# Seven block products for eight in the second MLP product of a two-layer trunk (one core, fp32 by hi/lo pairs)

## The chip, the cores and the metric

The kernel runs on one core of one Trainium2 chip. The metric is the time of one execution on the device, in microseconds, median of several runs.

## The reference, cut to what matters

A decoder trunk of two layers over 1024 tokens of width 1024, in float32. Layer 0 has a mixer (a linear recurrence beside stick-breaking attention), layer 1 a causal convolution module. Each layer ends in the MLP that the change is about; `D_FF` is 4096:

```
def sq_relu_mlp(h, w1, w2):
    a = jax.nn.relu(h @ w1)
    return (a * a) @ w2
...
        h = rms_norm(x, mlp_norm_g[layer])
        x = x + sq_relu_mlp(h, mlp_w1[layer], mlp_w2[layer])
```

The attention masks its strictly causal triangle by adding -1e30 to the scores of the diagonal block before the sigmoids.

## The kernel before, in words

**Precision.** Every large product is computed from operands split into a high part (`fp32r`, written by ScalarE's copy, lines 104 and 125) and a low part (source minus high part, VectorE's subtraction, lines 105 and 126). One product is then three matmuls: low x high, high x low, high x high (`mm3`, lines 157 to 159).

**Tiling.** The tokens go in two chunks of 512. The first MLP product (`m1`) takes a block `f` of 128 of the 4096 hidden columns: weights of two blocks come in one transfer of 1 MB (`col_units`, line 114), 8 blocks of depth with three matmuls each (24 matmuls, all 128x512) fill one PSUM bank, ScalarE applies relu and square (lines 252, 254, 255) and VectorE makes the low part (line 256). The result has hidden columns on the partitions and 512 tokens along the row. The second product (`m2`) takes groups of `G` = 4 hidden blocks and one half `h` of the 1024 output columns: 1 MB of `mlp_w2` (line 139), split in two pieces of 128x1024, and for each of the 4 token tiles 4 x 3 matmuls into one bank, which VectorE adds to the residual `x` (line 240). One MLP of one chunk is 32 `m1` and 16 `m2`, that is 768 + 768 matmuls. There are four: `a0` and `b0` (layer 0, chunks 0 and 1), `a1` and `b1` (layer 1).

**Buffers.** Pool `hp` has 48 slots of 128x512 (2 KB per partition); the residuals take 16 and the normed input of one chunk (high and low) 16. Pool `wp` has 2 slots for raw weights (8 KB), 4 for high and 4 for low parts (4 KB each). Pool `lp` (8 slots, 2.1 KB) is open throughout, `p1` belongs to the mixer and is followed in the same space by `p2` (tags `b` and `c`), which the rest of the kernel uses. PSUM has 8 banks: 2 for transposes (`ps`), and 6 in `ps1` (mixer) or `ps2` (4 `mm`, 2 `m1`).

**Order.** The kernel is written with a tile framework: the instructions are listed in program order, a list scheduler with its own model of times puts them in order on each engine and assigns buffer slots, and every semaphore wait follows from that. VectorE's depthwise convolution (480 instructions, line 648) is issued in small portions behind other VectorE work (`paced`); it lies beside `b0`, the convolution module and `a1`. The main order (lines 731 to 764) is: `m1` of `a0` twice, norm of chunk 1, the rest of `a0`, `b0` with the start of the convolution module, the convolution module of both chunks, `a1`, the norm of chunk 1, `finish(0)` (final norm and output of chunk 0), `b1`, `finish(1)`. All loads are issued from the SP queue. GpSimd issues none.

**Lines that the change touches:** pools (46, 600 to 609), identity and mask (74 to 81), `mlp` (243), the mask matmul (501), `finish` (704), the main order (730 to 764).

Of the kernel before, what the change touches and what calls it, by code (L numbers as in the profile page):

```python
# [15 lines left out]
P = 128  # L16
# [15 lines left out]
def tile_hybrid_trunk(  # L32
# [13 lines left out]
    lp = ctx.enter_context(tc.tile_pool(name="lp", bufs=8))  # L46
# [8 lines left out]
    def hf(name):  # L55
        return ht(name, F32)
# [2 lines left out]
        return ht(name, dt)  # L59

    def lt(name):
        return lp.tile([P, HALO + C], F32, tag="l", name=name)

    def mm_ps(name):
        return mmp[0].tile([P, C], F32, tag="mm", bufs=mmp[1], name=name)
# [11 lines left out]
    make_identity(nc, ident_b)  # L77
    mask = cp.tile([P, P], BF16, name="mask")
    Q.memset(mask, 0.0)
    Q.affine_select(out=mask, in_=mask, pattern=[[-1, P]], compare_op=ALU.is_gt,  # L80
                    fill=-1e30, base=0, channel_multiplier=1)

    cp.tile([P, 16], F32, name="pad_cp")
    mhalf = cp.tile([P, 1], F32, name="mhalf")
# [155 lines left out]
            paced(V.tensor_tensor(xt[t][h], acc, xt[t][h], op=ALU.add), 1.5)  # L240


    def mlp(layer, hT, xt, name):
# [20 lines left out]
        order = [(m1, f) for f in range(G)]  # L264
        for g in range(NG):
# [6 lines left out]
    NG = FF // (G * P)  # L272


    w_in = ev_w_in[0]
    y = [[None] * KT for _ in range(NCH)]
    dp = ctx.enter_context(tc.tile_pool(name="dp", bufs=1, space=bass.MemoryType.DRAM))
    with tc.tile_pool(name="p1", bufs=1) as p1, tc.tile_pool(name="ps1", bufs=1, space=PSUM) as ps1:
        mmp = (ps1, 2)

        def qt(name):
            return p1.tile([P, C], F32R, tag="q", bufs=8, name=name)
# [197 lines left out]
        def attention(c, hp, q1, q2, ks):  # L480
            av = ps1.tile([P, C], F32, tag="av", bufs=1, name=f"av{hp}{c}")
            order = None
            for tt in range(TT):
                n = (c * TT + tt + 1) * P
                carry = [None, None]
                hi_s = n
                while hi_s > 0:
                    lo_s = (hi_s - 1) // C * C
                    w = hi_s - lo_s
                    nb = w // P  # L490
                    diag = hi_s == n
                    wts = []
                    for j in range(2):
                        nm = f"{c}{hp}{tt}{j}{lo_s}"
                        z = ps1.tile([P, C], F32, tag="z", bufs=3, name=f"z{nm}")
                        ts_, k_ = slice(tt * P, (tt + 1) * P), ks[lo_s // C][j]
                        with tc.high_priority(offset=1000):
                            T.matmul(z[:, :w], q1[j][:, ts_], k_[:, :w], start=True, stop=False)
                            T.matmul(z[:, :w], q2[j][:, ts_], k_[:, :w], start=False, stop=not diag)
                            if diag:  # L500
                                T.matmul(z[:, w - P:w], ident_b, mask, start=False, stop=True)

                        ke = at(f"ke{nm}")
                        with tc.high_priority(offset=1000):
                            A.activation(ke[:, :w], z[:, :w], AF.Sigmoid, scale=-0.125)
                            A.activation(z[:, :w], z[:, :w], AF.Sigmoid, scale=0.125)
                        ini = 1.0 if diag else carry[j]
                        if diag:
                            Q.memset(ke[:, w:w + 1], 1.0)
                        else:  # L510
                            Q.tensor_copy(ke[:, w:w + 1], ini)
                        V.tensor_tensor_scan(ke[:, :w][:, ::-1], ke[:, :w][:, ::-1], ke[:, :w][:, ::-1],
                                             ini, op0=ALU.mult, op1=ALU.bypass)
                        if lo_s > 0:
                            carry[j] = sp.tile([P, 1], F32, tag="carry", bufs=6, name=f"ca{nm}")
# [81 lines left out]
        for h in range(NH):  # L597
            out_proj((1,), 1, h)

    p2 = ctx.enter_context(tc.tile_pool(name="p2", bufs=1))  # L600
    p2.tile([P, 96], F32, tag="pad", bufs=1, name="pad_p2")
    ps2 = ctx.enter_context(tc.tile_pool(name="ps2", bufs=1, space=PSUM))
    mmp = (ps2, 4)

    def bt(name, dt=F32):
        return p2.tile([P, C], dt, tag="b", bufs=11, name=name)

    def ct(name):
        return p2.tile([P, C], F32, tag="c", bufs=9, name=name)


    halo = cp.tile([P, KT, HALO], F32, name="halo")
# [89 lines left out]
        rows_into_x(s[kg * 4:kg * 4 + 4], ws, h, x[c], f"q2{c}{kg}{h}")  # L702

    def finish(c):
        fg = [ct(f"fg{c}{h}") for h in range(NH)]
        for h in range(NH):
            nc.sync.dma_start(fg[h], final_g[h * C:(h + 1) * C].rearrange("(a d) -> a d", a=1).to_broadcast((P, C)))
        for t in range(TT):
            o = [ct(f"fo{c}{t}{h}") for h in range(NH)]
# [24 lines left out]
    steps(a0)  # L734
# [59 lines left out]
```

## Time and profile before

| | |
|---|---|
| Time, median of 3 runs | 2208.8 us (2208.58 to 2209.05) |
| Time of the profiled execution | 2208.25 us |
| Its span (first to last instruction) | 2206.5 us |
| TensorE matmul busy | 2158.0 us (98%), 10180 matmuls |
| TensorE weight load busy (beside the matmuls) | 1764.2 us (80%) |
| VectorE busy | 1412.0 us (64%) |
| ScalarE busy | 957.6 us (43%) |
| GpSimd busy | 104.2 us (5%) |
| DMA | 199.24 MB, mean 90 GB/s |
| Mean granted TensorE clock | 0.993 |

Busy shares are means over stages with different limits. Matmuls are pipelined, so the time that one takes from its engine is read from the distance between the starts of two, not from its duration.

### The profile page before, as it was taken

The numbers are of one execution on the slowest core, as the hardware profiler recorded it, in microseconds if no ns is written. First come the engines' busy times: TensorE is split into PE (matmuls) and PEld (weight loads), VectorE is DVE, ScalarE is ACT, GpSimd is POOL, SyncE is SP. The second block draws the span as 40 slices with busy tenths as digits, with TensorE's granted clock in tenths as the row PEclk, the third lists the DMA queues.
The fourth block names the chain that finished last, engine by engine and source line by source line (L and its number), as shares of the span: only waits on it lengthen the run. The fifth ranks groups of instructions, "written<-read, shape, count | busy, mean of one in ns | idle before, by whom it ended". The sixth has DMA issues, their size and how long they took to land.

```text
span 2206.5 us, 25861 instructions
## 1 busy us (share of the span) xinstructions
PE 2158.0 (98%) x10180; PEld 1764.2 (80%) x10180; DVE 1412.0 (64%) x1934; ACT 957.6 (43%) x1513; POOL 104.2 (5%) x296
## 2 busy tenths in 40 slices
PE   7999888999999999999999999999999999999998
PEld 5877666788888888888888888788888888888887
DVE  5386868975433435489899664999896555444344
ACT  4466766645333334333333463333333535333332
POOL 1000000000000002000000000300000001000000
PEclk9999989999999999999999999999999999999999
DMA  4110102212323322332232222223232234222232
GB/s 161 58 54 24 53 25 91 101 59 78 100 90 99 110 96 92 109 96 96 91 100 96 96 96 83 86 95 100 87 103 91 94 105 144 96 96 96 96 96 76
DMA packets 172009, 199.24 MB, mean 90 GB/s; under 512 B 5648, under 2 KB 120688, under 8 KB 171888
## 3 DMA queue, kind: packets, MB, share of 16 engines
q1 hardware_dynamic: 171872, 197.59, 27.6%
q8 instruction: 80, 1.31, 0.2%
q14 instruction: 41, 0.34, 0.1%
q10 hardware_dynamic: 16, 0.00, 0.0%
HBM read 190.23 MB, written 7.34 MB: 90 GB/s over the span
## 4 chain that ended last, share of the span: by engine, by line
PE 91%; DVE 4%; ACT 3%; issue 1%; DMA 0%; POOL 0%; DVEq 0%; SPq 0%; POOLq 0%; ACTq 0%
PE m_a L157 5%; PE m_a L159 5%; PE o_a L159 5%; PE m_b L159 5%; PE m_a L158 5%; PE m_b L157 5%; PE o_a L157 5%; PE o_a L158 5%; PE m_b L158 5%; PE o_b L159 5%; PE o_b L157 5%; PE o_b L158 5%; PE av L529 1%; PE o_q L157 1%; PE o_q L158 1%; PE o_q L159 1%
## 5 line engine op out<-in xcount | busy, mean ns | idle before, releaser
L648 DVE SCALAR_TENSOR_TENSOR cv<-u,dwT,cv 128x512 f32<-128x512 f32 x480 | 340.6, 756 | 0.2
L157 PE MATMUL o_a<-wh_w2a,al_a 128*128 128x512 f32 x512 | 199.6, 390 | 0.0
L158 PE MATMUL o_a<-wl_w2a,ah_a 128*128 128x512 f32 x512 | 199.5, 390 | 0.0
L157 PE MATMUL o_b<-wh_w2b,al_b 128*128 128x512 f32 x512 | 199.4, 390 | 0.0
L159 PE MATMUL o_b<-wh_w2b,ah_b 128*128 128x512 f32 x512 | 199.4, 389 | 0.0
L158 PE MATMUL o_b<-wl_w2b,ah_b 128*128 128x512 f32 x512 | 199.3, 389 | 0.0
L159 PE MATMUL o_a<-wh_w2a,ah_a 128*128 128x512 f32 x512 | 198.9, 389 | 0.0
L125 ACT CAST wh_w1b<-raw_w1b 128x1024 fp32r<-128x1024 f32 x64 | 67.3, 1052 | 211.9 <-PE o_b L159 168.6
L125 ACT CAST wh_w1a<-raw_w1a 128x1024 fp32r<-128x1024 f32 x64 | 67.3, 1053 | 206.2 <-PE o_a L159 162.8
L105 DVE TENSOR_TENSOR wl_w2a<-raw_w2a,wh_w2a 128x1024 fp32r<-128x1024 f32 x64 | 78.3, 1224 | 121.9 <-ACT wh_w2a L104 121.9
L105 DVE TENSOR_TENSOR wl_w2b<-raw_w2b,wh_w2b 128x1024 fp32r<-128x1024 f32 x64 | 80.9, 1264 | 115.9 <-ACT wh_w2b L104 115.8
L240 DVE TENSOR_TENSOR xr<-o_a,xr 128x512 f32<-128x512 f32 x128 | 87.8, 688 | 76.5 <-PE o_a L159 76.1
L240 DVE TENSOR_TENSOR xr<-o_b,xr 128x512 f32<-128x512 f32 x128 | 88.0, 688 | 71.3 <-PE o_b L159 70.9
L252 ACT ACTIVATE r_a<-m_a 128x512 f32<-128x512 f32 x64 | 38.4, 599 | 170.5 <-PE m_a L159 170.5
L159 PEld LDWEIGHTS o_b<-wh_w2b,ah_b 128*128 128x128 f32 x512 | 96.1, 188 | 19.9
L158 PEld LDWEIGHTS o_b<-wl_w2b,ah_b 128*128 128x128 f32 x512 | 96.1, 188 | 19.9
L159 PEld LDWEIGHTS o_a<-wh_w2a,ah_a 128*128 128x128 f32 x512 | 96.1, 188 | 19.9
L157 PEld LDWEIGHTS o_a<-wh_w2a,al_a 128*128 128x128 f32 x512 | 96.1, 188 | 19.8
L158 PEld LDWEIGHTS o_a<-wl_w2a,ah_a 128*128 128x128 f32 x512 | 96.1, 188 | 19.8
L157 PEld LDWEIGHTS o_b<-wh_w2b,al_b 128*128 128x128 f32 x512 | 96.1, 188 | 19.8
L252 ACT ACTIVATE r_b<-m_b 128x512 f32<-128x512 f32 x64 | 38.4, 600 | 168.9 <-PE m_b L159 168.9
L126 DVE TENSOR_TENSOR wl_w1b<-raw_w1b,wh_w1b 128x1024 fp32r<-128x1024 f32 x64 | 78.0, 1221 | 36.0 <-ACT wh_w1b L125 35.6
(538 smaller groups left out, 5319.5 us busy)
## 6 DMA issues: line engine op xcount, KB each, us to landing
raw_w1a<-in_mlp_w_dram SPq DMA_DIRECT2D x32, 1024.0 KB, 5.1
raw_w2a<-in_mlp_w_dram SPq DMA_DIRECT2D x32, 1024.0 KB, 5.0
raw_w1b<-in_mlp_w_dram SPq DMA_DIRECT2D x32, 1024.0 KB, 5.1
raw_w2b<-in_mlp_w_dram SPq DMA_DIRECT2D x32, 1024.0 KB, 4.9
raw_pw<-in_od_pw_w_dram SPq DMA_DIRECT2D x32, 512.0 KB, 4.5
raw_q<-in_od_pw_w_dram SPq DMA_DIRECT2D x8, 1024.0 KB, 5.1
raw_wo<-in_ev_w_out_dram SPq DMA_DIRECT2D x6, 768.0 KB, 5.1
xa<-in_x_dram SPq DMA_DIRECT2D x16, 256.0 KB, 5.2
```

What stands on the lines that cost most here:

```text
L105: paced(V.tensor_tensor(lo, raw, hi.bitcast(F32), op=ALU.subtract), 1)
L125: A.copy(hi, srcs[i])
L126: paced(V.tensor_tensor(lo, srcs[i], hi.bitcast(F32), op=ALU.subtract), 2)
L157: T.matmul(acc, ll, rh, start=(i == 0), stop=False)
L158: T.matmul(acc, lh, rl, start=False, stop=False)
L159: T.matmul(acc, lh, rh, start=False, stop=(i == n - 1))
L240: paced(V.tensor_tensor(xt[t][h], acc, xt[t][h], op=ALU.add), 1.5)
L252: A.activation(r, acc, AF.Relu)
L529: ins = T.matmul(av[j * 64:j * 64 + 64, tt * P:(tt + 1) * P], vt[lo_s // P + b][:, hc:hc + 64], wts[j][:, b * P:(b + 1) * P], start=(diag ...
L648: waiting.append(lambda k=k, m=m: V.scalar_tensor_tensor(cv[m], u[m][:, k:k + C], dwT[:, k * KT + m:k * KT + m + 1], cv[m], op0=ALU.mult, ...
```

## The change

1. `mlp7` computes the second product of the MLP over eight hidden blocks at a time as a 2 x 2 x 2 block product with seven products instead of eight (a Strassen-Winograd scheme). The rows are the first and second 256 tokens of the chunk, the depth is the even and the odd hidden blocks, the columns are the two halves of the output. Each of the seven products is 2 token tiles x 4 depth blocks x 3 matmuls. It runs for three groups of `a0` (hidden blocks 0 to 23; the last 8 stay as they were, by `mlp(..., g0=6)`) and for all four groups of `b1`.
2. Sums of activation blocks (`s1` to `s4`) are made by VectorE, each then split high/low into slots of two wide tiles, `sh` and `sl`. Three sums of weight blocks are needed: `w11+w12`, `w12+w22` and `w11+w12+w22` are made by DMAs issued from GpSimd that add to a loaded tile (`accum_op`), and `w21` is added to the last of them by VectorE. Each operand is split while the product before runs (`ws`, `nx`).
3. Products accumulate in PSUM across products; after each one VectorE adds its bank to, or subtracts it from, one block of `x`.
4. Pools: `pa`/`psa` (strassen) replace `lp` + `p1`/`p2` and the `ps1`/`ps2` banks while they are open, so there are three changes of pools in place of one. `finish` takes its tiles from `hp`.
5. The identity and the mask are `fp32r` tiles, made through a float32 tile and a VectorE copy; the mask matmul is fp32r in place of bf16.

```diff
-    ident = cp.tile([P, P], F32, name="ident")
-    make_identity(nc, ident)
-    ident_b = cp.tile([P, P], BF16, name="ident_b")
-    mask = cp.tile([P, P], BF16, name="mask")
...
+    ident_r = cp.tile([P, P], F32R, name="ident_r")
+    ident = ident_r.bitcast(F32)
+    mask = cp.tile([P, P], F32R, name="mask")
+    for t_, fill in ((ident_r, None), (mask, -1e30)):
+        raw_c = wp.tile([P, P], F32, tag="wl", bufs=4, name="raw_c")
...
+        V.tensor_copy(t_, raw_c)
...
+    def mlp7(layer, hT, xt, name, pa, psa, groups):
+        w1, w2 = mlp_w1[layer], mlp_w2[layer]
+        def pair(f, n):
+            un = col_units(w1, f * P, (f + 1) * P, f"w1{n}")
+            lo = pa.tile([P, 7 * B2], F32R, tag="sl", bufs=4, name=f"sl{n}")
+            hi = pa.tile([P, 7 * B2], F32R, tag="sh", bufs=4, name=f"sh{n}")
+            ev, od, sa, sb = [hf(f"r{i}_{n}") for i in range(4)]
+            (a21, a11), (a22, a12), (s1, s3), (s2, s4) = [(r[:, :B2], r[:, B2:]) for r in (ev, od, sa, sb)]
+            def parts(r, s0):
+                sl = slice(s0 * B2, s0 * B2 + r.shape[1])
+                A.copy(hi[:, sl], r)
+                V.tensor_tensor(lo[:, sl], r, hi[:, sl].bitcast(F32), op=ALU.subtract)
+            for i, r in enumerate((ev, od)):
+                acc = m1_ps(f"m1_{n}{i}")
+                colmm(acc, un(i), hT)
+                A.activation(r, acc, AF.Relu)
+                A.activation(r, r, AF.Square)
+                if i == 0:
+                    V.tensor_tensor(s3, a11, a21, op=ALU.subtract)
+                    parts(a11, 0)
+            V.tensor_tensor(s1, a21, a22, op=ALU.subtract)
+            V.tensor_tensor(s2, s1, a11, op=ALU.subtract)
+            V.tensor_tensor(s4, a12, s2, op=ALU.add)
+            for r, s0 in ((od, 1), (sa, 3), (sb, 5)):
+                parts(r, s0)
+            return hi, lo
+        def w_rows(g, odd, h, nm):
...
+                t_ = hf(f"{nm}{name}{g}{k}")
+                nc.sync.dma_start(t_, w2[f * P:(f + 1) * P, h * C:(h + 1) * C])
...
+        def w_add(ts, g, odd, h):
+            for k in range(4):
+                f = 8 * g + 2 * k + odd
+                Q.dma_start(ts[k], w2[f * P:(f + 1) * P, h * C:(h + 1) * C], accum_op=ALU.add)
+        def w_split(ts, nm):
...
+                for j in range(2):
+                    js = slice(j * C, (j + 1) * C)
+                    A.copy(hi[:, js], ts[2 * i + j])
+                    V.tensor_tensor(lo[:, js], ts[2 * i + j], hi[:, js].bitcast(F32), op=ALU.subtract)
...
+        def product(banks, acts, slot, ws, first, into):
+            for t in range(2):
...
+                    T.matmul(banks[t], lo[:, ts], rh, ...)
+                    T.matmul(banks[t], hi[:, ts], rl, ...)
+                    T.matmul(banks[t], hi[:, ts], rh, ...)
+                for row, h, op in into:
+                    x_ = xt[(2 if row == 1 else 0) + t][h]
+                    V.tensor_tensor(x_, x_, banks[t], op=op)
...
+        for g in groups:
+            acts = [pair(8 * g + 2 * p, f"{n}{p}") for p in range(3)]
+            t1 = w_rows(g, 0, 0, "w11")
+            ws = w_split(t1, f"w11{n}")
+            w_add(t1, g, 0, 1)
+            t2 = w_rows(g, 1, 1, "t2")
+            w_add(t2, g, 0, 0)
+            w_add(t2, g, 0, 1)
+            acts.append(pair(8 * g + 6, f"{n}3"))
+            ba, bb = bank(f"pa_{n}", "sa"), bank(f"pb_{n}", "sb")
+            nx = w_split(t1, f"t1{n}")
+            w22 = w_rows(g, 1, 1, "w22")
+            product(ba, acts, 0, ws, True, [(1, 0, ALU.add)])
+            ws, nx = nx, w_split(t2, f"t2{n}")
+            t3 = w_rows(g, 0, 1, "w12")
+            w_add(t3, g, 1, 1)
+            product(bb, acts, 3, ws, True, [(2, 1, ALU.add)])
+            ws, nx = nx, w_split(w22, f"w22{n}")
+            w21 = w_rows(g, 1, 0, "w21")
+            product(ba, acts, 5, ws, False, [(1, 1, ALU.subtract)])
+            ws, nx = nx, w_split(t3, f"t3{n}")
+            for k in range(4):
+                V.tensor_tensor(t2[k], t2[k], w21[k], op=ALU.add)
+            product(bb, acts, 6, ws, False, [(1, 1, ALU.add)])
+            ws, nx = nx, w_split(w21, f"w21{n}")
+            product(ba, acts, 4, ws, False, [(2, 1, ALU.subtract)])
+            ws, nx = nx, w_split(t2, f"t4{n}")
+            bc = bank(f"pc_{n}", "sb")
+            product(bc, acts, 2, ws, True, [(1, 0, ALU.add)])
+            product(ba, acts, 1, nx, False, [(2, 0, ALU.add)])
...
-                                T.matmul(z[:, w - P:w], ident_b, mask, start=False, stop=True)
+                                T.matmul(z[:, w - P:w], ident_r, mask, start=False, stop=True)
...
-    a0 = mlp(0, hm[0], x[0], "a0")
+    strassen(0, hm[0], x[0], "a0", range(3))
+    mid = ExitStack()
...
+    a0 = mlp(0, hm[0], x[0], "a0", 6)
     steps(a0, -1)
...
     finish(0)
-    b1 = mlp(1, h2b, x[1], "b1")
-    steps(b1)
+    mid.close()
+    strassen(1, h2b, x[1], "b1", range(4))
     finish(1)
```

## Rows read from the trace of the kernel before

**Rows 1.** The page: span, busy time and instructions of each engine.
```profile
span 2206.5 us, 25861 instructions
PE 2158.0 (98%) x10180; PEld 1764.2 (80%) x10180; DVE 1412.0 (64%) x1934; ACT 957.6 (43%) x1513; POOL 104.2 (5%) x296
```

**Rows 2.** Stretches: us, busy us and (instructions) per engine, clock, DMA share, GB/s.
```profile
100.00:500.00 400.00, 377.51 (x2169) 290.81 (x2168) 308.19 (x451) 256.52 (x498) 23.77 (x126) 0.97 0.18 60
506.00:855.00 349.00, 348.28 (x1553) 288.77 (x1554) 147.19 (x175) 132.84 (x193) 4.70 (x12) 1.00 0.30 97
1850.00:2180.00 330.00, 330.00 (x1457) 273.27 (x1456) 135.33 (x155) 120.94 (x162) 3.25 (x6) 1.00 0.30 99
```

**Rows 3.** Waits of TensorE, 506 to 2190 us: total us, times, longest.
```profile
PE nps_ma L214 <- DVE hl_ma L220: 2.9, 2, 2.7
PE m_a L157 <- ACT hh_m L219: 0.9, 1, 0.9
```

**Rows 4.** TensorE's timeline in `b1`: start, duration, the 25 starts of one `m2` half.
```profile
1964.92 0.39 PE L157 MATMUL o_b<-wh_w2b,al_b 128*128 128x512 f32 x1
...
1970.36 0.39 PE L157 MATMUL o_b<-wh_w2b,al_b 128*128 128x512 f32 x1
```

**Rows 5.** VectorE and ScalarE by line, 1850 to 2190 us: count, busy us, mean ns.
```profile
L240 DVE TENSOR_TENSOR xr<-o_b,xr 128x512 f32<-128x512 f32 x60 | 41.4, 690 | 58.2 <-PE o_b L159 58.0
L126 DVE TENSOR_TENSOR wl_w1b<-raw_w1b,wh_w1b 128x1024 fp32r<-128x1024 f32 x30 | 36.6, 1221 | 25.1 <-ACT wh_w1b L125 25.1
L256 DVE TENSOR_TENSOR al_b<-r_b,ah_b 128x512 fp32r<-128x512 f32 x32 | 22.1, 691 | 27.6 <-ACT r_b L255 27.6
L254 ACT ACTIVATE ah_b<-r_b 128x512 fp32r<-128x512 f32 x32 | 20.1, 630 | 0.2
```

**Rows 6.** VectorE by line, the whole span: a tensor_tensor of 256 columns.
```profile
L517 DVE TENSOR_TENSOR ke<-z,ke 128x256 f32<-128x256 f32 x16 | 6.6, 421 | 1.1
```

**Rows 7.** VectorE's timeline in `b1`, around the start at 1964.92 of an `m2`.
```profile
1950.96 1.23 DVE L105 TENSOR_TENSOR wl_w2b<-raw_w2b,wh_w2b 128x1024 fp32r<-128x1024 f32 x1 [4.92 <-ACT wh_w2b L104]
1955.81 1.23 DVE L105 TENSOR_TENSOR wl_w2b<-raw_w2b,wh_w2b 128x1024 fp32r<-128x1024 f32 x1 [2.96 <-ACT wh_w2b L104]
1967.84 0.69 DVE L240 TENSOR_TENSOR xr<-o_b,xr 128x512 f32<-128x512 f32 x1
1968.45 0.68 DVE L256 TENSOR_TENSOR al_b<-r_b,ah_b 128x512 fp32r<-128x512 f32 x1
```

**Rows 8.** The page: DMA issues, KB each, median us from issue to landing.
```profile
raw_w2b<-in_mlp_w_dram SPq DMA_DIRECT2D x32, 1024.0 KB, 4.9
xa<-in_x_dram SPq DMA_DIRECT2D x16, 256.0 KB, 5.2
out_dram<-fo SPq DMA_DIRECT2D x16, 256.0 KB, 2.0
```

**Rows 9.** TensorE's timeline in the mixer: the mask matmul, and eight fp32 transposes.
```profile
439.29 0.34 PE L499 MATMUL z<-ks,q 128*128 128x384 f32 x1
439.47 0.23 PE L501 MATMUL z<-mask,ident_b 128*128 128x128 bf16 x1
439.51 0.47 PE L498 MATMUL z<-ks,q 128*128 128x512 f32 x1
494.84 1.03 PE L214 MATMUL nps_m<-ident,xn_m 128*128 128x128 f32 x8
495.63 0.48 PE L157 MATMUL o_wo<-wh_wo,y13l 128*128 128x512 f32 x1
```

**Rows 10.** Weight loads in the mixer, by line: count, busy us, mean ns.
```profile
L498 PEld LDWEIGHTS z<-ks,q 128*128 128x128 f32 x96 | 18.8, 196 | 9.6 <-DVE ks L564 3.8 <-DVE ke L517 2.3 <-PE z L499 0.6
L501 PEld LDWEIGHTS <-ident_b 128*128 128x128 bf16 x64 | 6.3, 99 | 7.6 <-issue 6.8
```

**Rows 11.** The end of the chain of waits: start, us, engine, tile, line.
```profile
2190.61 0.24 PE o_b L159
2190.88 0.70 DVE xr L240
...
2199.07 0.67 DVE xr L240
2199.82 0.63 ACT fo L186
```

More of the change, by code (lines that the diff above doesn't have):

```diff
@@ L61, in lt @@
     def lt(name):
-        return lp.tile([P, HALO + C], F32, tag="l", name=name)
+        return lpp[0].tile([P, HALO + C], F32, tag="l", bufs=8, name=name)
     def mm_ps(name):
@@ L71, in tr_ps @@
         return ps.tile([P, C], F32, tag="tr", bufs=2, name=name)
-    ident = cp.tile([P, P], F32, name="ident")
-    make_identity(nc, ident)
-    ident_b = cp.tile([P, P], BF16, name="ident_b")
-    make_identity(nc, ident_b)
-    mask = cp.tile([P, P], BF16, name="mask")
-    Q.memset(mask, 0.0)
-    Q.affine_select(out=mask, in_=mask, pattern=[[-1, P]], compare_op=ALU.is_gt,
-                    fill=-1e30, base=0, channel_multiplier=1)
+    ident_r = cp.tile([P, P], F32R, name="ident_r")
[3 more added lines that the diff above has]
+        raw_c = wp.tile([P, P], F32, tag="wl", bufs=4, name="raw_c")
+        if fill is None:
+            make_identity(nc, raw_c)
+        else:
+            Q.memset(raw_c, 0.0)
+            Q.affine_select(out=raw_c, in_=raw_c, pattern=[[-1, P]], compare_op=ALU.is_gt,
+                            fill=fill, base=0, channel_multiplier=1)
+        V.tensor_copy(t_, raw_c)
     cp.tile([P, 16], F32, name="pad_cp")
@@ L240, in rows_into_x, with mlp @@
             paced(V.tensor_tensor(xt[t][h], acc, xt[t][h], op=ALU.add), 1.5)
-    def mlp(layer, hT, xt, name):
+    def mlp(layer, hT, xt, name, g0=0):
         acts, units = {}, {}
@@ L263, in mlp @@
         NF = FF // P
-        order = [(m1, f) for f in range(G)]
-        for g in range(NG):
+        order = [(m1, f) for f in range(g0 * G, (g0 + 1) * G)]
+        for g in range(g0, NG):
             n = (g + 1) * G
@@ L272, in tile_hybrid_trunk, with bank @@
     NG = FF // (G * P)
+    B2 = 2 * P
+    def mlp7(layer, hT, xt, name, pa, psa, groups):
[25 more added lines that the diff above has]
+        def w_rows(g, odd, h, nm):
+            ts = []
+            for k in range(4):
+                f = 8 * g + 2 * k + odd
+                t_ = hf(f"{nm}{name}{g}{k}")
+                nc.sync.dma_start(t_, w2[f * P:(f + 1) * P, h * C:(h + 1) * C])
+                ts.append(t_)
+            return ts
+        def w_add(ts, g, odd, h):
+            for k in range(4):
+                f = 8 * g + 2 * k + odd
+                Q.dma_start(ts[k], w2[f * P:(f + 1) * P, h * C:(h + 1) * C], accum_op=ALU.add)
+        def w_split(ts, nm):
+            res = []
+            for i in range(2):
+                hi = wp.tile([P, 1024], F32R, tag="wh", bufs=4, name=f"wh_{nm}{i}")
+                lo = wp.tile([P, 1024], F32R, tag="wl", bufs=4, name=f"wl_{nm}{i}")
+                for j in range(2):
+                    js = slice(j * C, (j + 1) * C)
+                    A.copy(hi[:, js], ts[2 * i + j])
+                    V.tensor_tensor(lo[:, js], ts[2 * i + j], hi[:, js].bitcast(F32), op=ALU.subtract)
+                    res.append((hi[:, js], lo[:, js]))
+            return res
+        def product(banks, acts, slot, ws, first, into):
+            for t in range(2):
+                ts = slice(slot * B2 + t * P, slot * B2 + (t + 1) * P)
+                for i, ((hi, lo), (rh, rl)) in enumerate(zip(acts, ws)):
+                    T.matmul(banks[t], lo[:, ts], rh, start=(first and i == 0), stop=False, skip_group_check=not first)
+                    T.matmul(banks[t], hi[:, ts], rl, start=False, stop=False, skip_group_check=not first)
+                    T.matmul(banks[t], hi[:, ts], rh, start=False, stop=(i == 3), skip_group_check=not first)
+                for row, h, op in into:
+                    x_ = xt[(2 if row == 1 else 0) + t][h]
+                    V.tensor_tensor(x_, x_, banks[t], op=op)
+        def bank(nm, tag):
+            return [psa.tile([P, C], F32, tag=tag, bufs=2, name=f"{nm}{t}") for t in range(2)]
+        for g in groups:
+            n = f"{name}{g}"
+            acts = [pair(8 * g + 2 * p, f"{n}{p}") for p in range(3)]
[18 more added lines that the diff above has]
+            ws, nx = nx, w_split(t3, f"t3{n}")
+            for k in range(4):
+                V.tensor_tensor(t2[k], t2[k], w21[k], op=ALU.add)
[6 more added lines that the diff above has]
+            product(ba, acts, 1, nx, False, [(2, 0, ALU.add)])
@@ L277, in tile_hybrid_trunk @@
     dp = ctx.enter_context(tc.tile_pool(name="dp", bufs=1, space=bass.MemoryType.DRAM))
-    with tc.tile_pool(name="p1", bufs=1) as p1, tc.tile_pool(name="ps1", bufs=1, space=PSUM) as ps1:
+    lpp = [None]
+    with tc.tile_pool(name="lp1", bufs=1) as lp1, tc.tile_pool(name="p1", bufs=1) as p1, \
+            tc.tile_pool(name="ps1", bufs=1, space=PSUM) as ps1:
         mmp = (ps1, 2)
+        lpp[0] = lp1
         def qt(name):
@@ L598, in tile_hybrid_trunk @@
             out_proj((1,), 1, h)
[L600 to L603, printed above, removed]
+    pp = [None]
     def bt(name, dt=F32):
-        return p2.tile([P, C], dt, tag="b", bufs=11, name=name)
+        return pp[0].tile([P, C], dt, tag="b", bufs=11, name=name)
     def ct(name):
-        return p2.tile([P, C], F32, tag="c", bufs=9, name=name)
+        return pp[0].tile([P, C], F32, tag="c", bufs=9, name=name)
     halo = cp.tile([P, KT, HALO], F32, name="halo")
@@ L704, in finish @@
     def finish(c):
-        fg = [ct(f"fg{c}{h}") for h in range(NH)]
+        fg = [hf(f"fg{c}{h}") for h in range(NH)]
         for h in range(NH):
@@ L708, in finish @@
         for t in range(TT):
-            o = [ct(f"fo{c}{t}{h}") for h in range(NH)]
+            o = [hf(f"fo{c}{t}{h}") for h in range(NH)]
             rs = rstd_of(x[c][t], o[0], f"f{c}{t}")
@@ L730, in tile_hybrid_trunk, with strassen @@
     hm.append(None)
-    a0 = mlp(0, hm[0], x[0], "a0")
+    def strassen(layer, hT, xt, name, groups):
+        nonlocal mmp
+        with tc.tile_pool(name=f"pa{name}", bufs=1) as pa, tc.tile_pool(name=f"psa{name}", bufs=1, space=PSUM) as psa:
+            mmp = (psa, 2)
+            pa.tile([P, 96], F32, tag="pad", bufs=1, name=f"pad_{name}")
+            mlp7(layer, hT, xt, name, pa, psa, groups)
+    strassen(0, hm[0], x[0], "a0", range(3))
+    mid = ExitStack()
+    lpp[0] = mid.enter_context(tc.tile_pool(name="lp2", bufs=1))
+    pp[0] = mid.enter_context(tc.tile_pool(name="p2", bufs=1))
+    pp[0].tile([P, 96], F32, tag="pad", bufs=1, name="pad_p2")
+    mmp = (mid.enter_context(tc.tile_pool(name="ps2", bufs=1, space=PSUM)), 4)
+    a0 = mlp(0, hm[0], x[0], "a0", 6)
     steps(a0, -1)
```

1 line of the change is left out of this document (removed).

## The prediction

> **What bounds the kernel now.** I read the page's first lines, then the stretches, then TensorE's waits, then single rows for the prices. TensorE is busy for 98% of the span [rows 1], but a busy matmul engine can hide pauses, so the stretches decide: the two stages that the change rewrites, `a0` (506 to 855 us) and `b1` (1850 to 2180 us), have TensorE busy for 348.28 of 349.00 and 330.00 of 330.00 us, at a granted clock of 1.00 [rows 2], which is the 2.4 GHz level. The reader should see beside it that VectorE is busy for 147 and 135 us there, ScalarE for 133 and 121, GpSimd for 5 and 3: 40% at most. The waits agree: from 506 to 2190 us TensorE waits twice, 3.8 us in all [rows 3]. So in both stages the time is the count of matmuls times their distance. That distance is (1970.36 - 1964.92) / 24 = 0.2267 us [rows 4]; the duration of 0.39 us in the same rows is not it. What the change takes from TensorE there it takes from the end, as long as the other engines and the transfers keep up.
>
> **The change part by part.** *Matmuls.* Eight hidden blocks cost 2 x 2 x 4 x 4 x 3 = 192 matmuls in `m2`; seven products cost 7 x 2 x 4 x 3 = 168. They have the same shape and operands of the same type, so I price them the same. Seven groups save 7 x 24 = 168 matmuls, 168 x 0.2267 = **-38.1 us**. All of it lies on the path. The count should read 10180 - 168 = 10012.
>
> *VectorE and ScalarE in a group.* TensorE needs (192 + 168) x 0.2267 = 81.6 us for a group, 43.5 for the first products and 38.1 for the seven products, 5.44 for each. VectorE has per group 8 low parts of `w1` (1.22 us each), 28 of 128x512 for weights and 12 for activations (0.69), 4 of 256 columns, 16 sums of 256 columns (0.42), 14 adds into `x` (0.69) and 4 for the last weight sum (0.69) [rows 5, 6]: 9.8 + 27.6 + 1.7 + 6.7 + 9.7 + 2.8 = 58.3 us of 81.6. The share rises from 41% to 71%, still hidden on average. Inside the seven products it is tighter: 28 + 14 + 4 operations of 0.69 are 31.7 us, the sums and low parts of the last pair 3 x 0.42 + 3 x 0.69 = 3.3, the first two `w1` units of the next group 2.4: 37.5 of 38.1 us. Durations overlap a little (one starts 0.61 us after the start of another that lasts 0.69 [rows 7]); at 0.63 instead of 0.69 it is 34.6, 91%. ScalarE does 28 copies of 0.63 = 17.6 us and about 5 us for the last pair and the next group's first units. What gives slack: of four pieces of a weight operand the first product of a bank needs the first at once and the last only after 9 matmuls (2.0 us), and the buffers for the next operand come free as soon as the product before has ended. One operand is ready about 0.63 + 4 x 0.69 = 3.4 us after that, within 5.44. I charge seams, where the last pair's sums, the first operands and the adds into `x` queue on VectorE together: between 0 and 3 us per group (3 is roughly the pile of that pair). Nearest is the low end, since the activations of the last pair are needed only after 9 of 12 matmuls; I take 1.0, **+7 us** (0 to 21).
>
> *Adding DMAs.* The trace shows neither one nor any transfer issued from GpSimd. Each adds 256 KB of weights to a tile; there are 4 for `w11+w12`, 8 for the triple sum (two rounds on the same tiles, so the second round waits for the first to land), 4 for `w12+w22`. GpSimd is idle here, so nothing else queues behind them, but they are in order on its queue. The window: before, the two pieces of an `m2` operand were ready at 1952.19 and 1957.04 for a first use at 1964.92 [rows 4, 7], because four buffers allow that much lead. `w11` will be split about as early, and only then may `w12` be added to it. The triple sum is wanted for the third product, whose split has to begin about 1.2 us before 1964.92 + 2 x 5.44, at 1974.6. So from 1957.0 there are 17.6 us for what is queued, and the triple sum's first four need not wait for the split: 8 remain. Per add, 1.25 us if 256 KB move at the rate of the 1 MB load (4.9 us), 2.5 if both operands count, 5.2 if each took the time to landing of a lone 256 KB load and they took turns; a 256 KB store lands in 2.0 [rows 8]. With a landing of 2 us after the last issue: 8 x 1.25 + 2 = 12, hidden with 5.6 us to spare; 8 x 2.5 + 2 = 22, late by 4.4; 8 x 5.2 + 2 = 43.6, late by 26. The row nearest to four adds in flight together is the 1 MB load, so I take 1.25 and **0 us** (0 to 31, far more at the last end). The traffic is no limit: a group moves 4 MB of `w1`, 5 MB of `w2` and 4 MB added, 13 MB or 17 with the read-back, in 82 us, about 210 GB/s, against 1 MB in 4.9 us.
>
> The Trainium skill, "DMA: Bandwidth & Descriptors", section "Anatomy of one DMA — SWDGE (gpsimd) path", gives a transfer issued from GpSimd about 2.0 us plus its bytes at 436 GB/s, an estimate of 2.6 us for 256 KB. [...]
>
> *Pools.* There are three changes of pools instead of one. If the first bank of the new pool waits for the last add into `x` (0.69 us, plus hand-overs), TensorE pauses about 1.2 us; the present change costs 0.9, and for another reason [rows 3]. **+3 us** (0 to 6). `pa` itself is first written 5.4 us into the first product, so its space is not waited for.
>
> *Mask.* 64 matmuls of 128 columns change from bf16 to fp32r. Now the next matmul starts 0.04 us behind one; eight fp32 transposes of that shape go at 0.79 / 8 = 0.10 each [rows 9]; and a weight load takes 0.196 instead of 0.099 us [rows 10]. So 0.06 more each, at most 0.196 - 0.04 = 0.16: 3.8 us, at most 10. In the mixer TensorE is busy for 94% [rows 2], so most of it counts: **+3 us** (0 to 10).
>
> *At nothing:* the identity's extra copy (needed later than the first loads); `finish(0)` in other slots, beside `b1`; the norm of chunk 1, which moves behind the three groups and lies beside the rest of `a0`, 8 `m1` and 4 `m2` or 87 us, as it lay beside `m1` before; more SP issues (20 loads of 256 KB and 4 of 1 MB a group instead of 8 of 1 MB, on a queue that does nothing else). If that cover went, one first product would be late, about 5 us. The end stays: from the last matmul to the last instruction some 7.6 us [rows 11], since again one token tile's add comes last.
>
> **Sum.** -38.1 + 7 + 0 + 3 + 3 = -25.1 on the execution's 2208.25 us (span 2206.5): 2183.2. The median of the runs is 0.55 higher, so **2184 us**.
>
> **The rivals.** *A: the adds are late.* Place: the third product of each group, TensorE waiting for the triple sum's high part; behind it ScalarE's later copies and the next operands queue, so nothing catches up. Price by the add: at 2.5 us it is 4.4 x 7 = 31 us, 2215; if in addition all twelve adds wait behind the split of `w11` on the queue, 12 x 2.5 + 2 - 17.6 = 14.4 per group, 2285. It passes the old time where a group loses more than 25.1 / 7 = 3.6 us, that is from (17.6 + 3.6 - 2) / 8 = 2.4 us per add. The same happens if slots are short: of 48 in `hp` 32 are taken, and two operands (8), one pair (4) and the next operand (4) fill the other 16; a late load shortens the window. For it: two operands per add, and an unseen resource on the path of every group. Against: 4 adds to different tiles do not wait for each other, and 1 MB lands in 4.9 us.
>
> *B: VectorE sets the pace of the products.* At 0.69 us per operation it has 37.5 of 38.1 us, and hand-overs from ScalarE (its low part always waits for the copy) leave gaps; if a group's products take 3 us longer, 21 instead of 7 us: 2198. For it: the 98%; against: the pipelined starts.
>
> *C: no gain.* The list scheduler orders for its own times; if its order of loads and adds costs 3.6 us a group, the time is about 2209. The matmul count would still fall, so this is the way in which the change would fail to do what it says.
>
> **How the numbers follow.** About 0.2% (4.4 us) is what measurement can tell from no change. Forecast 0.53, with its own range of 2171 (every cost at zero) to 2194; B 0.13, faster; C 0.08, of which I count 0.07 as within 0.2%; A 0.26, slower. So faster 0.66, same 0.07, slower 0.27. The range runs from 2171 to 2230: it leaves out the far half of A and little below.
>
> **What would show it.** 10012 matmuls; TensorE's waits in the two stages below 2 us per group; the first products at 0.2267 us. A shows as TensorE idle at the third product, released by ScalarE's copy of the triple sum and that by a DMA from GpSimd's queue; B as waits on VectorE's low parts spread over all products with VectorE over 95% in the products; the mask as less than 10 us more in the mixer. The prediction is wrong if an add takes over 2.4 us from its queue, or if TensorE pauses more than 3.6 us in each group.

## The result, and the profile after

The changed kernel takes 2256.6 us (median, 2254.5 to 2258.7), the kernel before 2208.7 in the same comparison: ratio 1.0213, 95% interval 1.0202 to 1.0225. It is slower by 48 us; 2184 was forecast and 2230 was the upper end of the range. The profiled execution took 2254.7 us.

The page, first lines; compare [rows 1]:

```profile
span 2252.9 us, 26544 instructions
PE 2146.7 (95%) x10012; PEld 1751.9 (78%) x10012; DVE 1534.5 (68%) x2258; ACT 1039.2 (46%) x1709; POOL 206.9 (9%) x406
```

The 168 matmuls are gone as announced, and yet the span has grown by 46.4 us. TensorE's busy share fell from 98 to 95%: it now waits. Where, the stretches say (columns as in [rows 2]: us, busy us and count of PE, PEld, DVE, ACT and POOL, granted clock, DMA share, GB/s). The first row answers to the second of [rows 2]; the others follow one group of `b1`:

```profile
506.00:855.00 349.00, 324.71 (x1396) 265.20 (x1397) 192.71 (x303) 158.35 (x261) 48.15 (x61) 0.96 0.51 136
1882.00:1975.00 93.00, 86.74 (x364) 70.74 (x363) 52.83 (x86) 42.25 (x69) 14.21 (x16) 0.94 0.57 147
2000.00:2003.00 3.00, 2.20 (x5) 1.70 (x6) 2.89 (x6) 3.00 (x6) 1.15 (x2) 0.50 0.00 0
...
2006.00:2024.00 18.00, 17.83 (x79) 14.44 (x77) 4.17 (x7) 5.19 (x10) 6.40 (x8) 1.00 1.07 228
...
2027.00:2030.00 3.00, 3.00 (x9) 2.37 (x8) 2.75 (x6) 2.15 (x4) 0.75 (x2) 0.54 1.05 397
```

In the stretch of `a0` TensorE is busy for 324.71 us; it was 348.28. The group's short rows show the second half of the loss: after a pause the granted clock is 0.50 to 0.54, TensorE's lower level (1.2 GHz), for some microseconds, and then 1.00 again. VectorE, rival B's engine, has 52.83 of 93 us.

The pauses themselves, from TensorE's timeline (start, duration; in brackets the idle time before and who ended it):

```profile
2000.80 1.22 PE L346 MATMUL pa_b<-wh_w11b,slb 128*128 128x512 f32 x2 [4.38 <-ACT wh_w11b L336]
2001.82 0.63 PE L347 MATMUL pa_b<-wl_w11b,shb 128*128 128x512 f32 x1
2002.25 0.63 PE L348 MATMUL pa_b<-wh_w11b,shb 128*128 128x512 f32 x1
...
2023.22 0.39 PE L347 MATMUL pb_b<-wl_t1b,shb 128*128 128x512 f32 x1
2023.45 0.39 PE L348 MATMUL pb_b<-wh_t1b,shb 128*128 128x512 f32 x1
2025.94 0.47 PE L346 MATMUL pa_b<-wh_t2b,slb 128*128 128x512 f32 x1 [2.10 <-DVE xr L351]
```

Starts are 0.43 us apart behind a pause (2001.82, 2002.25) and 0.23 at full clock (2023.22, 2023.45; 0.2267 in [rows 4]). I summed what the distances of starts from 1974.50 to 2067.08 have above 0.2267: the first pause costs 4.54 us, the second 2.26, and 22 matmuls at wide distances 4.14 (with the rest of the group, 10.97 in all). The groups are not alike: the same sum gives 14.1, 10.9 and 9.4 us for those of `a0` and 11.1, 11.0, 10.8 and 7.1 for those of `b1`. The seven lose 74.4 us, 48.6 of them in pauses and some 24 at wide distances.

A short pause is not always followed by the lower level. This one in `a0`, 2.6 us by the distances of starts, is not (the timeline, and below it the stretch around it, at a granted clock of 1.00):

```profile
665.49 0.47 PE L346 MATMUL pa_a<-wh_t2a,sla 128*128 128x512 f32 x1 [2.39 <-DVE xr L351]
```

```profile
662.00:668.00 6.00, 3.61 (x16) 2.67 (x15) 5.31 (x10) 4.81 (x9) 0.60 (x1) 1.00 1.07 339
```

In the seven groups the eight pauses of more than 4 us are all followed by the lower level, and of the seven shorter ones (1.0 to 2.6 us) three are.

TensorE's waits, 500 to 2240 us, in the form of [rows 3] (us in total, times, longest):

```profile
PE pa_b L346 <- ACT wh_w11b L336: 13.1, 3, 4.4
PE pa_a L346 <- ACT wh_w11a L336: 8.8, 2, 4.4
PE pa_a L346 <- DVE xr L351: 6.7, 2, 4.3
PE pa_a L346 <- issue: 4.4, 1, 4.4
...
PE pa_b L346 <- DVE xr L351: 3.9, 2, 2.1
...
PE pa_b L346 <- DVE slb L297: 2.0, 1, 2.0
```

Seven times up to 4.4 us before the first product: five times under ScalarE's split of `w11` (first two rows) and twice under "issue", where no releaser was seen (the second of these rows is like the one shown). The rows with `xr` at L346 are the second pause in four groups. In two more it stands under the parts of the last pair's activations (`slb`, and rows like it for `sla` and `sha`), and the last group of `b1` has none.

**Why the first operand is late.** Three queues in the same group: SP's issues, ScalarE, and GpSimd's issues.

```profile
1961.41 16.48 SPq L117 DMA_DIRECT2D raw_w1b<-in_mlp_w_dram  x3
1977.98 2.20 SPq L319 DMA_DIRECT2D w11b<-in_mlp_w_dram  x4
...
1996.46 0.60 ACT L302 ACTIVATE r_b<-m_b 128x512 f32<-128x512 f32 x1 [3.73 <-PE m_b L162]
...
1999.61 0.62 ACT L296 CAST shb<-r_b 128x512 fp32r<-128x512 f32 x1 [0.72 <-DVE r_b L309]
2000.13 1.66 ACT L336 CAST wh_w11b<-w11b 128x512 fp32r<-128x512 f32 x3
...
2001.85 2.65 POOL L327 DMA_DIRECT2D w11b<-in_mlp_w_dram  x3 [60.56 <-DVE wl_w11b L337]
2003.59 4.46 POOL L327 DMA_DIRECT2D t2b<-in_mlp_w_dram  x4
```

On SP the loads of `w11` stand behind a load of `w1` that waits for its buffer until 1977.9. On ScalarE the split of `w11` starts at 2000.13, behind the whole third pair of `r` (its last cast at 1999.61), although the data landed at 1983.6 (chain below). ScalarE was not short of time: before 1996.46 it was idle for 3.73 us, waiting for the matmuls of that pair's second hidden block. What held the split was its place in ScalarE's order. And GpSimd, idle for 60.56 us, starts its first twelve adds only when `w11` has been split. The chain of waits for that group tells the same and leads to the second pause:

```profile
1977.98 5.63 DMA w11b<-in_mlp_w_dram
1983.67 18.16 issue
...
2004.13 10.48 DMA t2b<-in_mlp_w_dram
...
2015.14 8.69 DMA t2b<-in_mlp_w_dram
2023.85 0.63 ACT wh_t2b L336
2024.50 0.69 DVE wl_t2b L337
2025.19 0.61 DVE xr L351
```

For the piece of the triple sum that the chain follows, the two adds, one in each round, take 10.48 and 8.69 us to landing and end at 2023.83. The third product waits for a sum into `x` (`xr`) that frees its bank; that sum stands on VectorE behind the low part of the triple sum. So one late transfer blocks work that had been ready.

### The profile page after: what moved, and what is told of

Read it like the earlier page. It is cut to its first block, busy times and chain, and to the rows that moved or that the text cites. A ratio compares the mean times of both kernels' runs of the same rounds, so it can differ in the third digit from the quotient of the medians.

```text
span 2252.9 us, 26544 instructions
## 1 busy us (share of the span) xinstructions
PE 2146.7 (95%) x10012; PEld 1751.9 (78%) x10012; DVE 1534.5 (68%) x2258; ACT 1039.2 (46%) x1709; POOL 206.9 (9%) x406
## 4 chain that ended last, share of the span: by engine, by line
PE 75%; issue 8%; DMA 7%; DVE 5%; ACT 3%; POOL 1%; SPq 0%; POOLq 0%; DVEq 0%; ACTq 0%
PE m_a L160 4%; PE m_a L161 4%; PE m_a L162 4%; PE o_a L160 3%; PE o_a L161 3%; PE o_a L162 3%; PE m_b L160 3%; PE m_b L162 3%; PE m_b L161 3%; DMA t2a<-in_mlp_w_dram 3%; PE o_b L162 3%; PE o_b L161 3%; PE o_b L160 3%; DMA w11b<-in_mlp_w_dram 2%; DMA t2b<-in_mlp_w_dram 2%
## 5 line engine op out<-in xcount | busy, mean ns | idle before, releaser
L160 PE MATMUL m_a<-hh_m,wl_w1a 128*128 128x512 f32 x256 | 99.7, 390 | 2.5 <-DVE xr L351 1.6
L160 PE MATMUL m_b<-hh_mb,wl_w1b 128*128 128x512 f32 x256 | 99.7, 390 | 0.8 <-DVE xr L243 0.8
L160 PE MATMUL m_a<-hh_ma,wl_w1a 128*128 128x512 f32 x256 | 100.3, 392 | 0.0
L162 PE MATMUL m_b<-hh_m,wh_w1b 128*128 128x512 f32 x256 | 100.1, 391 | 0.0
L160 PE MATMUL m_b<-hh_m,wl_w1b 128*128 128x512 f32 x256 | 99.9, 390 | 0.0
L161 PE MATMUL m_a<-hl_ma,wh_w1a 128*128 128x512 f32 x256 | 99.9, 390 | 0.0
L162 PE MATMUL m_a<-hh_ma,wh_w1a 128*128 128x512 f32 x256 | 99.9, 390 | 0.0
L161 PE MATMUL m_b<-hl_m,wh_w1b 128*128 128x512 f32 x256 | 99.8, 390 | 0.0
L162 PE MATMUL o_b<-wh_w2b,ah_b 128*128 128x512 f32 x256 | 99.8, 390 | 0.0
L162 PE MATMUL m_a<-hh_m,wh_w1a 128*128 128x512 f32 x256 | 99.8, 390 | 0.0
```

The source lines that it names most:

```text
L160: T.matmul(acc, ll, rh, start=(i == 0), stop=False)
L161: T.matmul(acc, lh, rl, start=False, stop=False)
L162: T.matmul(acc, lh, rh, start=False, stop=(i == n - 1))
```

## The experiments

Theory **order**: the adds have bandwidth enough, but loads, splits and adds stand too late in the engines' orders. Rival **adds**: the adding transfers themselves are too slow. Diffs are against the changed kernel unless said otherwise.

**1. The adds left out.** The sums then hold one block each; all else stays.

```diff
-                Q.dma_start(ts[k], w2[...], accum_op=ALU.add)
+                pass
```

> The changed kernel without its adding DMAs (the three weight sums are left out: the operands are w11, w22 and w12 alone). In the changed kernel each of the seven groups takes some 92.6 us where 360 matmuls at 0.2267 us are 81.6: about 4.4 us of pause before the first product, where ScalarE's split of w11 stands behind all the work of the third pair, some 2.3 us more because the matmuls after the pause run at half clock, about 2.2 us of pause before the third product and 1.5 us at half clock after it. Theory 'order': only the second pause belongs to the adds, so 7 x 3.7 = 26 us go and the time is about 2230. Theory 'adds' (rival A as predicted: the adds hold up every group and nothing else does): all 77 us go, about 2180.

Measured: 2223.2 us, ratio to before 1.0061 (1.0045 to 1.0078). The second pause is gone, the first stays seven times. Without a single add the kernel is still slower than before; the time is near the 2230 of theory order and far from the 2180 of theory adds. The rows under `slb`, `sla` and `sha` are gone too, so those pauses also need the adds. The first of its rows of waits, three of the seven first pauses, is that of the change:

```profile
PE pa_b L346 <- ACT wh_w11b L336: 13.1, 3, 4.4
```

**2. The loads and the triple sum ahead of the group's first pair.** The split of `w11` and the add of `w12` to it stay behind the third pair in the source.

```diff
-            acts = [pair(8 * g + 2 * p, f"{n}{p}") for p in range(3)]
+            acts = [pair(8 * g + 2 * p, f"{n}{p}") for p in range(0)]
             t1 = w_rows(g, 0, 0, "w11")
-            ws = w_split(t1, f"w11{n}")
-            w_add(t1, g, 0, 1)
             t2 = w_rows(g, 1, 1, "t2")
             w_add(t2, g, 0, 0)
             w_add(t2, g, 0, 1)
+            acts += [pair(8 * g + 2 * p, f"{n}{p}") for p in range(0, 3)]
+            ws = w_split(t1, f"w11{n}")
+            w_add(t1, g, 0, 1)
-            acts.append(pair(8 * g + 6, f"{n}3"))
+            acts += [pair(8 * g + 2 * p, f"{n}{p}") for p in range(3, 4)]
```

> The changed kernel with the loads of w11 and w22 and the triple sum's adds written ahead of the group's first pair, the split of w11 and the adding of w12 left after the third pair; nothing is added or removed. Theory 'order': the split of w11 is placed ahead of the third pair's work on ScalarE, the first pause goes (7 x 6.7 = 47 us), and with it most of the second, since the adds begin some 15 us earlier: 2180 to 2190, faster than the kernel before (2208.7). Theory 'adds' (their rate is too low for the group, wherever they begin): the second pause stays or grows into the first one's room, 2230 to 2256.

Measured: 2179.7 us, 0.9867 (0.9852 to 0.9882). Every add is still there and the kernel is 29 us faster than before, 77 faster than the change as it was. The stretch of `b1`, and below it TensorE's waits from 506 us on:

```profile
1840.00:2160.00 320.00, 320.00 (x1411) 264.24 (x1410) 205.64 (x342) 159.91 (x268) 58.67 (x69) 1.00 0.64 166
```

```profile
PE nps_ma L217 <- DVE hl_ma L223: 2.9, 2, 2.6
PE m_a L160 <- DVE xr L351: 1.6, 1, 1.6
PE m_b L160 <- DVE xr L243: 0.8, 1, 0.8
```

No product waits; the clock is 1.00. In one group `w11` is split from 1935.6 on for a first use at 1951.06, its last two pieces from 1940.9: about the lead that the prediction had assumed.

**3. Both: early, and without adds** (experiment 2's order with experiment 1's edit; the sums again hold one block).

> As the run with the early loads, and without the adding DMAs (the three weight sums are left out). Both theories: no pause left, 2180 (the count of matmuls, 168 x 0.2267 us less than before, and about 9 us of other costs or less). The difference to the run with the early loads and the adds is what the adds still cost once they begin early: theory 'order' 0 to 5 us, theory 'adds' 26 us or more.

Measured: 2175.8 us, 0.9848 (0.9834 to 0.9863). With 1, 2 and the change this makes a square. Without adds the order is worth 2223.24 - 2175.76 = 47.5 us, 6.8 a group: the pause of 4.5 and the slow matmuls behind it. With the early order the adds cost 3.9 us in all, 3.5 of them at the very end of the span (experiment 10). With the late order they cost 33.3: it is the start that makes them dear. A late add also takes longer: the page's median from issue to landing of the triple sum's adds is 9.1 us (`b`) and 9.5 (`a`) in the change and 6.2 in experiment 2; the late ones stand in stretches with a DMA share above 1, against 0.64 on average in experiment 2. How much of this is due to the plain loads beside them was not tried.

**4. One pair earlier is enough?** As 2, but behind two pairs instead of none (`range(2)`, then `range(2, 3)`).

> As the run with the early loads, but the loads and the triple sum stand only one pair earlier than in the changed kernel (ahead of the third pair instead of behind it). In the built order three of the four pieces of w11 are split before the third pair's results reach ScalarE. Theory 'order': the first pause goes here too; the adds begin about 11 us earlier instead of 15, so the second pause may stay in part: 2183 to 2205. Theory 'adds': 2230 to 2256.

Measured: 2181.0 us, 0.9871 (0.9856 to 0.9886), no wait in the products. The pools are those of the change, so a want of slots is not the cause. The lead of one pair, 10.9 us of matmuls (43.5 / 4), is enough.

**5. Only the loads of `w11` one pair earlier,** and **6. only the triple sum** (its loads and eight adds) one pair earlier.

```diff
-            acts = [pair(8 * g + 2 * p, f"{n}{p}") for p in range(3)]
+            acts = [pair(8 * g + 2 * p, f"{n}{p}") for p in range(2)]
             t1 = w_rows(g, 0, 0, "w11")          # 6: t2's four lines here instead
+            acts.append(pair(8 * g + 4, f"{n}2"))
```

> The changed kernel with the four loads of w11 alone written one pair earlier (ahead of the third pair); the loads of w22, all splits and all adds stay where they are in the program. In the built order the split of w11 then stands ahead of the third pair's work on ScalarE, for all but one piece. Theory 'order' (one late split of one operand starts everything): the first pause goes, and the adds start as much earlier: 2180 to 2190. Rival 'two causes' (the triple sum is late for its own sake, since its tile is still loaded late): the first pause goes, the second stays: 2256.6 - 47 = about 2210.

> The complement of the run in which w11 alone is loaded early (2232): here the load of w22 and the triple sum's two rounds of adds stand ahead of the third pair, and the load, split and add of w11 stay where the changed kernel has them. In the built order the split of w11 again stands behind the third pair's work on ScalarE. Theory 'two causes' (a late split in front of the first product, and a late triple sum in front of the third, each with its own pause and half clock after it): the first pause of 4.4 us stays in all seven groups, the second goes, and the time is that of the run without adds, 2220 to 2230. Theory 'order' as first put (the late split alone starts everything): nothing is gained, about 2250.

Measured: 2232.3 us (1.0101; 1.0086 to 1.0117) and 2226.1 (1.0076; 1.0059 to 1.0093). Each takes away its own pause: 6 still has the first, seven times 4.4 us; 5 has only the second, which has grown (six times, 4.6 to 7.9 us; the third row is one of 4.6 under `wh_t2a`). The 2226.1 of 6 is what two separate causes were to give; for 5 neither expectation came true. TensorE's waits in 5, and below them the chain of one group:

```profile
PE pa_b L346 <- DVE xr L351: 20.2, 3, 7.5
PE pa_a L346 <- DVE xr L351: 13.5, 2, 7.9
```

```profile
1985.96 1.23 DVE wl_w1b L129
...
1987.64 5.48 DMA t2b<-in_mlp_w_dram
...
1993.65 7.32 DMA t2b<-in_mlp_w_dram
...
2001.50 7.53 DMA t2b<-in_mlp_w_dram
```

A load and one add of each round, 21.4 us in a row from 1987.64 to 2009.03 for the first piece (the fourth is ready at 2014.4), and the row starts late: the load stood on SP's queue behind one of `w1` that waited for VectorE to release a buffer (1985.96, 1.23 us). The gains of 5 and 6 are 24.2 and 30.4 us, those of both together 75.6: with the first pause gone alone, TensorE only comes sooner to a triple sum that is still late.

**7. Twice the adds, early.** Experiment 2 with each add issued twice, so the sums hold one operand twice.

```diff
                 Q.dma_start(ts[k], w2[...], accum_op=ALU.add)
+                Q.dma_start(ts[k], w2[...], accum_op=ALU.add)
```

> The run with the early loads, each adding DMA issued twice, the second behind the first on the same tile (the sums then hold one operand twice). It asks how much room the adds have once they start early. At 2.1 us per add, as in the changed kernel, 32 adds take 67 us of a group's 82. Theory 'room': they begin some 30 us ahead of the triple sum's use, where 24 adds and four rounds now stand, about 50 us: late by some 20 us in each group, 2320 or more. Rival (the 2.1 us were due to plain loads running beside them, an add by itself takes about 1 us): no more than 5 us per group, 2180 to 2215.

Measured: 2196.1 us, 0.9943 (0.993 to 0.9957), still faster than before. The 2320 of theory 'room' is far off; the time lies in the rival's range, though its reason, the loads beside the adds, is not shown by it. The 112 more adds (16 in each of seven groups) cost 16.4 us, 0.15 each; the longest pause is one on the last sum, `w12+w22`, with one landing right ahead of it on the chain, which ends at 1912.90 (waits, then chain):

```profile
PE pa_b L347 <- ACT wh_t3b L337: 6.6, 1, 6.6
```

```profile
1904.27 8.62 DMA w12b<-in_mlp_w_dram
```

So sixteen adds a group have room, and thirty-two begin not to.

**8. The sums by VectorE instead,** with all loads one pair earlier, as in 4: no adding DMA, 16 more VectorE sums per group, all loads plain.

```diff
-            w_add(t2, g, 0, 0)
-            w_add(t2, g, 0, 1)
+            for k in range(4):
+                V.tensor_tensor(t2[k], t2[k], t1[k], op=ALU.add)
```

(and likewise `w11+w12`, `t2+w12`, `w12+w22`)

> Loads early (w11, w22 and w12 ahead of the third pair), and the three weight sums made by VectorE (16 more additions of 128x512 per group) instead of the adding DMAs; the sums are the same. VectorE gets 16 x 0.69 = 11 us more in a group of 82, on top of 53 measured. Theory 'VectorE has room': 2176 to 2186, like the adding DMAs started early. Rival B of the prediction (VectorE sets the pace): pauses of 1 to 3 us per group, 2187 to 2205.

Measured: 2181.9 us, 0.9878 (0.9865 to 0.9891). That is 2.2 us above 2 and 0.9 above 4. VectorE takes 11 us more a group and only half a microsecond of it shows at TensorE (this row four times, a like one of `pa_a` three times):

```profile
PE pa_b L346 <- DVE xr L351: 2.0, 4, 0.5
```

The near equality has two parts. The last matmul starts 4.6 us later than in 2 (2167.93 against 2163.37), and from the last sum of a product to the end of the span it is 11.8 us instead of 15.2, for the reason found in 10.

**9. The mask alone,** on the kernel before.

```diff
-                                T.matmul(z[:, w - P:w], ident_b, mask, start=False, stop=True)
+                                T.matmul(z[:, w - P:w], ident_r, mask, start=False, stop=True)
```

(with the identity and the mask as fp32r tiles)

> The kernel before with the fp32r identity and mask alone. By the prediction's step +3 us (0 to 10): 2211 to 2212. Rival, from the trace of the changed kernel, where the first product of the MLP starts at 505.99 instead of 506.72 us: nothing, 2208 to 2209.

Measured: 2206.7 us, 0.9989 (0.998 to 0.9998). It costs nothing; the interval leaves 0.4 to 4.4 us of gain, so the time is even a little below the rival's 2208 to 2209.

**10. The end.** In the change the last sum of a product into `x` starts at 2237.47, and the span ends 15.4 us later; in the kernel before it was 7.4 ([rows 11], 2199.07 to 2206.5). Its chain of waits there:

```profile
2237.47 0.70 DVE xr L351
...
2238.94 1.35 ACT fo L189 x4
...
2240.31 0.73 ACT fo L189 x2
```

Each square on ScalarE is followed by an instruction that reads its sum, so x4 is two squares. Six squares come after the last sum, of which the chain has four (one at 2238.19); the expectation below says eight. The final norm takes the token tiles in the order 0, 1, 2, 3, while the last product adds into 0 and 1. On top of experiment 2, the order was turned:

```diff
-    finish(1)
+    finish(1, (2, 3, 0, 1))
```

(and `finish` goes through the token tiles in the order that it is given)

> The early order of e2, and in the last finish the token tiles whose last sum comes first (2 and 3) are normed first, 0 and 1 last. If the longer end (15.2 us from the last sum of a product to the end of the span in e2, 7.4 in the kernel before) comes from ScalarE's eight squares standing behind the last product in the wrong order of token tiles, some 3 to 6 us of it go: 2174 to 2177 us, the end 9 to 12 us. If the end is fixed by the last product's own sums and the stores, it stays: 2179 to 2181 us.

Measured: 2176.1 us, 0.985 (0.9837 to 0.9864), the fastest kernel here that leaves nothing out, and 3.6 below experiment 2 (the two intervals overlap; the traces show the gain where the edit acts). Its chain at the end:

```profile
2162.44 0.70 DVE xr L351
...
2163.16 0.73 ACT fo L189 x2
...
2163.91 0.63 ACT fo L189
```

Two squares instead of six, and 11.3 us instead of 15.2 (2163.80 to 2179.0 in experiment 2).

The rest of the longer end is not in the norm. VectorE's last instructions, in experiment 2 and below in experiment 3, which has no adds:

```profile
2171.20 1.41 DVE L828 SCALAR_TENSOR_TENSOR fo<-xr,rs_f,fg 128x512 f32<-128x512 f32 x2 [0.44 <-POOL rs_f L192]
```

```profile
2169.30 1.41 DVE L828 SCALAR_TENSOR_TENSOR fo<-xr,rs_f,fg 128x512 f32<-128x512 f32 x2 [0.44 <-POOL rs_f L192]
```

They end at 2172.61 and 2170.71, the spans at 2179.0 and 2173.6: 6.4 us against 2.9. In the traces it is 6.4 to 6.6 us in the six kernels with 112 adds and 2.9 in the five without. The last to end there is a closing DRAIN on GpSimd, 8.05 us long in experiment 2 (2170.19 to 2178.24) and 1.05 in experiment 3. With twice the adds (7) it is 2.05 and the stretch 3.0, so the number of adds does not set it; what does is open.

## Why the prediction was wrong

*Matmuls, -38.1 us: right.* 10012, at 0.23 us from start to start wherever the clock is 1.00. Experiment 2 keeps the whole gain: its stretch of `b1` is busy for 320.00 of 320.00 us.

*Adding DMAs, 0 us: this step failed,* and in it the sentence "`w11` will be split about as early". The lead in [rows 7] came from the four buffers and from an order in which the split of `w2` stood well ahead of its use. In the change the split of `w11` stands behind the third pair, on ScalarE, and its load behind a blocked load on SP. The product was to start 7.9 us after its operand was ready; it waits 4.4 us for it. With that the window of 17.6 us for the queued adds is gone too, and the four adds that "need not wait for the split" do wait: on GpSimd's queue they stand behind the adds to `w11` (2003.59 behind 2001.85). I had taken the lead for a property of the buffers; it is one of the program's order. Experiments 2 and 4 show it: the same adds, earlier, and no wait is left in the products.

The size of an add was put too low as well, but it is not what decided. From the first issue to the last landing twelve adds take 26 us (2001.85 to about 2027.8), or 2.0 each by the prediction's own form with 2 us of landing; in experiment 5 eight take 20.7 (1993.65 to about 2014.4), or 2.3. Both lie above my 1.25 and below the break-even of 2.4; at 2.3 the predicted window alone would have been missed by 3.1 us a group. With the early order adds of this kind cause no wait. And landing is no 2 us: the adds on the chains above take 7.3 to 10.5 from issue to landing, while those of the second round in experiment 5 land 1.3 to 2.1 us apart, so several are in flight together. The Trainium skill, "DMA: Bandwidth & Descriptors", section "Anatomy of one DMA — SWDGE (gpsimd) path", has a fit that gives an estimate of 2.6 us for a lone one, and says that the wait for the receipt is most of its fixed 2.0 us. Four such in turns would be an estimate of 10.4 us; no run here has a lone add.

*The clock, priced nowhere.* Every pause of more than 4 us and three of the shorter ones are followed by matmuls at the lower level: some 24 us in seven groups beside 48.6 of pauses, against the 48 us by which the kernel is slower. No rival carried it. The Trainium skill, "TensorE: Matmul & The Clock Gate", section "What's actually happening", has the gate with two levels and ties it to how busy the engine has been. The same page of the Trainium skill, section "Wait — 56ns, not 53.3ns?", gives 426.7 and 215.7 ns as distances of starts; here they are 0.43 and 0.2267 us, so the slow one agrees, the fast one is 11 ns longer, and the sums here go by the measured one.

*VectorE and ScalarE, +7 us: too high.* The time in a group (52.83 us in that stretch, against 58.3) and the conclusion, that the work lies beside the matmuls, were right; in experiment 2 the seams cost less than 1 us in all seven groups, and in 8, with 11 us more, about 0.5 a group.

*Pools, +3 us: right.* 1.6 and 0.8 us (`m_a` behind `xr`, `m_b` behind `xr`), 2.4.

*Mask, +3 us: wrong;* it costs nothing, and the interval lies just below the range (0 to 10).

*The end, "stays" at 7.6 us: wrong by 8.* I had seen that one token tile's add comes last again, and not that the norm takes the tiles in another order than they are finished in. Of the 8.0 us more, 4.2 lie between the last sum and VectorE's last instruction (8.8 against 4.6), and experiment 10 gets 4.0 of these back; the other 3.8 lie behind it, where GpSimd's closing DRAIN ends last.

*Rivals.* A had the side, the second pause's place (the third product, in five of seven groups) and one of its clauses ("all twelve adds wait behind the split of `w11`"). It did not have the first pause, which is larger and needs no add: experiment 1. That is C's mechanism (the order of loads and adds costs some microseconds a group), which I priced at 3.6 us and 8 in 100; both pauses and the clock together are 10.6 a group here. B did not happen.

The sum with measured terms: -38.1 - 0 + 74.4 (pauses and lower clock) + 2.4 (pools) + 8.0 (end) = +46.7, against +46.4 in the spans. For experiment 2: -38.1 + 2.4 + 7.8 = -27.9, against -27.5. That experiment 2 lands 4 us from the forecast of 2184 is in part luck: the end, priced at nothing, took most of what was set aside for seams and mask.

## What to carry to other kernels

When an operand passes from a buffered loop into a written-out sequence, its lead does not come along: read from each engine's order where its load, its split and whatever is chained to it will stand, and put the head of the longest chain (here load, two rounds of adds, split: 23 us) into the source that much ahead of the use. Price a pause of TensorE of some 4 us at its length plus the matmuls at half clock behind it, here 12 to 13 of them and 2.5 us; behind a shorter one they may or may not come. And where the order in which results are finished changes, change the order of whoever consumes them last.

## What the runs showed of the hardware

After some pauses of only 2.0 to 2.3 us the granted clock stood near 0.5 (0.54 in the stretch from 2027 on), and after one of 2.6 us it stayed at 1.00; 22 matmuls of the group shown stood at wide distances behind its two pauses. For the adding DMAs from GpSimd, 256 KB each with others in flight, the page's medians from issue to landing are 6.1 to 9.5 us in the change and 4.5 to 7.8 in experiment 2. Started early, the 112 of them cost the kernel 3.9 us, and 3.5 of these lie behind VectorE's last instruction, under a closing DRAIN on GpSimd of 8.05 us. VectorE did the same sums with its last matmul 4.6 us later and a DRAIN of 1.05 us, so that the two times lie close together (2181.9 and 2179.7 us).
